# A two-layer RWKV/short-convolution and conformer backbone: where the context stages write their gate and receptance projections

## The chip, the cores and the metric

The kernel runs on one core of one Trainium2 chip. The metric is device time in microseconds (us) for one execution, taken as the median of several runs. A core has engines that each run their own queue in order: TensorE (PE in the profile, with its weight loads shown as PEld), VectorE (DVE), ScalarE (ACT), GpSimd (POOL) and SyncE (SP). In this kernel PE does the matrix products, DVE and ACT the elementwise work, and SP and POOL issue nearly all the transfers from memory.

## The reference, cut to what matters

There are 256 context tokens and 512 latent tokens of width 1024. Layer 0 normalises both, multiplies them with one wide matrix `ev_w_in` (eight blocks of 1024 columns: r, k, v, za, bg, cg, xb, zb), runs a bidirectional RWKV-7 recurrence over the context and then, from its final states, over the latent tokens, and joins that with a gated short convolution. Layer 1 is a conformer convolution module on the latent tokens alone.

```
rc, kc, vc, zac, bc, cc, xc, zbc = split(hc @ w_in)      # context
yac, S_f, S_b = rwkv_seq(prep(hc, rc, kc, vc), 0, 0)     # only the final states are used
r, k, v, za, bg, cg, xb, zb = split(h @ w_in)            # latent tokens
ya, _, _ = rwkv_seq(prep(h, r, k, v), S_f, S_b)
yb = bg * dwconv(cg * xb, sc_w)
y = concat(ya * silu(za), yb * silu(zb)) @ w_out
```

Of the context only k and v are needed (its outputs are thrown away). Of the latent tokens all eight blocks are needed; r and za are the two that the change moves.

## The kernel before

The recurrence is computed in chunks of 64 tokens. Inside a chunk a triangular system is inverted; between chunks a 64x64 state per head and direction is carried. Everything is float32, and a projection is made of three products of rounded halves (`mm3`), eight steps deep, so one latent projection of 128 columns by 512 tokens is 24 matmuls of 128x512, and one context projection is 24 of 128x256.

Layer 0 is a pipeline of twelve states. `sts[0]` to `sts[3]` are the context, two pairs of heads (a pair is 128 channels) in each; `sts[4]` to `sts[11]` are the latent tokens, one pair in each. For each `s` the kernel first writes the chain of `sts[s]` (`chain_ctx`, four steps, or `chain_lat`, eight steps: PE products `zo` and `uh`, ACT copies, a DVE update of the state H) and then the steps that prepare the next states, in the order of a string:

```
for x in STAGE[s >= 4]:
    if x == "S":
        solve(sts[s + 1])
    elif x == "M":
        merge(sts[s + 1])
    ...
    elif x == "P" and s < 10:
        sts.append(prep_ctx(s + 2) if s < 2 else prep_lat(s - 2))
    elif x == "L" and s < 10:
        light(sts[s + 2], st)
    elif x == "H" and s < 10:
        heavy(sts[s + 2], st)
    elif x == "F":
        fills(s + 1)
```

- **P** (`prep_ctx`, L391 and after): the keys and values of two pairs, for context (`pck`, `pcv`) and latent tokens (`plk`, `plv`) in one go, four context and four latent projections per stage. For a latent state (`prep_lat`) it is only loads of what was stored before.
- **L** (`light`): decay, in-context rate and normalised keys: short products (`ss`, `lw`, `la`), some eighteen DVE operations on 128x512 and as many on ACT, two passes, one for each direction z.
- **S** (`solve`): the inverse of the 32x32 diagonal blocks, 62 small DVE operations (L667, L669).
- **M** (`merge`): joins the 32x32 blocks to 64x64 with 64 small products (`uh`), two DVE transposes and copies. Its scratch tiles are the buffers `kd`, `a`, `P` of `light`, each with one copy, so a merge stands behind the `light` written before it.
- **H** (`heavy`): the products of a chunk with itself (`pac`, `pal`), masked by DVE (L610) into the tile E; transposed keys (`pbc`, `pbl`) and values (`pvc`, `pvl`) copied out by ACT.
- **F** (`fills`): the projections that nothing nearby needs: r (`plr`, which also has two DVE shifts) and za (`pza`, an ACT tanh at L802 and a DVE product at L803). `FILL_R` and `FILL_Z` fix which pair goes to which stage: `fills(1)` is za of pairs 1 to 3, `fills(2)` r of pair 2, `fills(3)` r of pair 3 and za of pairs 4 to 7, `fills(4)` r of pairs 4 to 7. Results are stored to memory and read back much later.
- **O**: `po`, for a latent state only.

Each half of a projection's weights is loaded by SP (256 KB), rounded by ACT (L128) and subtracted by DVE (L129) before PE can use it.

A scheduler in the framework lays the instructions of all engines out from the written order: what is written earlier has precedence, and later work is put into gaps where it expects the earlier to wait. So the written order is a ranking; the queues that come out of it are fixed when the program is built. The state `s` whose chain follows is written after all of this stage's steps.

Of the kernel before, what the change touches and what calls it, by code (L numbers as in the profile page):

```python
# [31 lines left out]
CONV_AFTER = (0, 2, 7, 6)  # L32
PA_ORDER = ((0, 1), (1, 0), (1, 1), (0, 0))
HEAVY = ("VBOAN", "ANBV")
STAGE = ("OFPLSMH", "OSPLMHFC")
FILL_R = (0, 0, 2, 3, 4, 4, 4, 4)
FILL_Z = (0, 1, 1, 1, 3, 3, 3, 3)
ZR = (slice(0, 64), slice(64, 128))
# [13 lines left out]
def kernel(ctx: ExitStack, tc: tile.TileContext, I: dict, out: bass.AP):  # L52
# [876 lines left out]
    for s in range(12):  # L929
# [7 lines left out]
        if s == 11:  # L937
            finish(st)
            break
        for x in STAGE[s >= 4]:  # L940
            if x == "S":
# [397 lines left out]
```

## Time and profile before

| | |
|---|---|
| median of 3 runs | 1439.53 us (1431.3 to 1440.98) |
| the profiled execution | 1434.6 us, span of its core 1432.5 us |
| PE busy | 1376.7 us, 96% |
| DVE busy | 983.0 us, 69% |
| ACT busy | 749.5 us, 52% |
| mean granted clock of PE | 0.982 |

The context stages lie between about 217 us and 525 us of the span, the latent stages of layer 0 from there to about 950 us, and then the output projection and layer 1, which keep PE full. A busy PE is no sign of PE at full speed: where the granted clock (row PEclk) is 0.50, the same matmul takes twice as long and counts as busy throughout.

### The profile page before, as it was taken

How to read it: one execution, taken by the hardware profiler on the slowest of the kernel's cores; microseconds unless marked ns; L12 is line 12 of the kernel's file. 1: busy time of each engine (PE TensorE's matmuls, PEld its weight loads, DVE VectorE, ACT ScalarE, POOL GpSimd, SP SyncE). 2: the span in 40 equal slices, each digit the busy share in tenths (PEclk: the TensorE clock that was granted, in tenths of full speed). 3: DMA queues.
4: the chain of work that ended last, by engine and by line, in shares of the span. 5: the costliest groups of instructions: out<-in, count | busy, mean ns of one | idle time of the engine just before them, and what ended most of it. 6: DMA issues, size and time to landing. Idle time of an engine off the chain costs nothing.

```text
span 1432.5 us, 29756 instructions
## 1 busy us (share of the span) xinstructions
PE 1376.7 (96%) x11921; PEld 1008.3 (70%) x11921; DVE 983.0 (69%) x2294; ACT 749.5 (52%) x1516; POOL 117.9 (8%) x246
## 2 busy tenths in 40 slices
PE   6899999999998998999999999999999999999998
PEld 1464677878776766666666666778777777788886
DVE  2675597568678989999999999656745545544333
ACT  4636355254555666756667565456753423464322
POOL 2023210000101101011010100010000000000000
PEclk9999999979898999999999999999999999999999
DMA  9754433222322221222222312358813303133322
GB/s 322 226 177 161 156 111 97 92 60 61 93 87 75 82 81 60 77 75 71 83 77 68 98 43 92 110 174 321 265 45 118 119 9 109 59 100 92 103 89 88
DMA packets 137626, 158.54 MB, mean 111 GB/s; under 512 B 15375, under 2 KB 104143, under 8 KB 137369
## 3 DMA queue, kind: packets, MB, share of 16 engines
q1 hardware_dynamic: 121104, 106.47, 23.7%
q0 software_dynamic: 15312, 48.99, 10.5%
q8 instruction: 94, 1.54, 0.4%
q10 hardware_dynamic: 1072, 1.19, 0.2%
q14 instruction: 44, 0.36, 0.1%
HBM read 138.33 MB, written 18.28 MB: 109 GB/s over the span
## 4 chain that ended last, share of the span: by engine, by line
PE 63%; DVE 14%; ACT 5%; issue 2%; DMA 0%; DVEq 0%; ACTq 0%
PE pu L57 12%; PE pz L57 6%; PE f L57 6%; PE o L57 5%; PE uh L57 4%; PE zol L57 4%; PE pcg L57 3%; PE pxb L57 3%; PE pza L57 3%; DVE E L610 2%; PE plk L57 2%; PE zoc L57 2%; PE pzb L57 2%; PE plv L57 1%; PE pac L57 1%
## 5 line engine op out<-in xcount | busy, mean ns | idle before, releaser
L57 PE MATMUL o<-wh,y 128*128 128x512 f32 x248 | 79.6, 397 | 0.0
L667 DVE TENSOR_TENSOR xtmpl<-Xl,Yl 128x126 f32<-128x126 f32 (+22 forms) x248 | 62.3, 251 | 2.8
L669 DVE TENSOR_TENSOR Yl<-Yl,xtmpl 128x126 f32<-128x126 f32 (+22 forms) x248 | 62.3, 251 | 2.7
L1152 ACT CAST ah<-a 64x512 fp32r<-64x512 f32 x32 | 19.8, 619 | 72.2 <-DVE a L1147 71.8
L57 PE MATMUL pal<-ARl,BKl 64*128 64x128 f32 x512 | 46.3, 300 | 10.7 <-DVE E L610 4.9
L57 PE MATMUL zol<-UV,E 64*64 64x64 f32 (+1 forms) x1024 | 54.2, 221 | 0.0
L57 PEld LDWEIGHTS o<-wh,y 128*128 128x128 f32 x248 | 45.9, 188 | 9.5
L57 PEld LDWEIGHTS pal<-ARl,BKl 64*128 64x128 f32 x512 | 36.4, 194 | 22.2 <-issue 7.2
L57 PE MATMUL zol<-Hl,ARl 64*64 64x64 f32 x896 | 50.2, 230 | 1.2 <-DVE Hl L782 1.0
L775 ACT COPY UV<-uh 64x128 f32<-64x128 f32 x128 | 33.2, 260 | 33.1 <-PE uh L57 25.6
L57 PE MATMUL o<-wl,y 128*128 128x512 f32 x124 | 49.4, 398 | 1.2 <-DVE wl L129 1.2
L57 PEld LDWEIGHTS zol<-Hl,ARl 64*64 64x64 f32 x896 | 35.0, 133 | 21.2 <-issue 17.0
L129 DVE TENSOR_TENSOR wl<-wr,wh 128x1024 fp32r<-128x1024 f32 x28 | 34.2, 1222 | 19.7 <-ACT wh L128 17.0
L57 PEld LDWEIGHTS uh<-UV,BKt 128*64 128x64 f32 x704 | 26.3, 137 | 28.7 <-ACT UV L775 23.0
L1147 DVE TENSOR_TENSOR a<-pu,a 128x512 f32<-128x512 f32 x16 | 11.0, 690 | 50.5 <-PE pu L57 48.2
L57 PEld LDWEIGHTS zol<-UV,E 64*64 64x64 f32 (+1 forms) x1024 | 42.4, 136 | 2.8 <-ACT UV L775 2.1
L610 DVE TENSOR_TENSOR E<-pal,maskE 128x512 f32<-128x512 f32 x64 | 42.9, 685 | 2.0 <-PE pal L57 1.2
L1107 DVE SCALAR_TENSOR_TENSOR pr<-px,dbe,What 119x512 f32<-119x512 f32 x32 | 22.6, 746 | 26.8 <-PE px L57 26.8
L782 DVE SCALAR_TENSOR_TENSOR Hl<-uh,PCl,HPl 128x64 f32<-128x64 f32 x112 | 26.5, 277 | 19.5 <-PE uh L57 8.6
L128 ACT CAST wh<-wr 128x1024 fp32r<-128x1024 f32 x28 | 29.6, 1056 | 19.7 <-DMA wr<-in_ev_w_out_dram 10.3
L886 POOL DMA_DIRECT2D mwr<-in_mod_w_dram x56 | 29.8, 537 | 112.8 <-PE uh L57 67.7
L57 PE MATMUL uh<-UV,BKt 128*64 128x64 f32 x704 | 36.3, 232 | 2.5 <-ACT UV L775 2.5
(947 smaller groups left out, 4230.9 us busy)
## 6 DMA issues: line engine op xcount, KB each, us to landing
mwr<-in_mod_w_dram POOLq DMA_DIRECT2D x56, 256.0 KB, 3.5
wr<-in_ev_w_out_dram SPq DMA_DIRECT2D x28, 512.0 KB, 5.1
ectx<-in_mod_w_dram SPq DMA_DIRECT2D x12, 512.0 KB, 5.2
wrk<-in_ev_w_in_dram SPq DMA_DIRECT2D x16, 256.0 KB, 3.1
wrv<-in_ev_w_in_dram SPq DMA_DIRECT2D x16, 256.0 KB, 4.1
wrr<-in_ev_w_in_dram SPq DMA_DIRECT2D x16, 256.0 KB, 2.7
wrza<-in_ev_w_in_dram SPq DMA_DIRECT2D x16, 256.0 KB, 2.8
wrcg<-in_ev_w_in_dram SPq DMA_DIRECT2D x16, 256.0 KB, 2.8
```

Of the source, the lines that this page charges most:

```text
L57: return T.matmul(o, lhsT, rhs, start=start, stop=stop)
L128: S.copy(hi, raw)
L129: env["lo"].tensor_tensor(out=lo, in0=raw, in1=hi, op=ALU.subtract)
L610: st["ev"].append(V.tensor_tensor(out=E[:, h, z * NLAT + c0 : z * NLAT + c0 + m, :], in0=pas[h], in1=maskE[:, z * (1 + h) : z * (1 + h) + ...
L667: V.tensor_tensor(out=tv, in0=X[:, :i, i : i + 1].to_broadcast([P, i, m]), in1=Y[:, i : i + 1, c0:].to_broadcast([P, i, m]), op=ALU.mult)
L669: V.tensor_tensor(out=Y[:, :i, c0:], in0=Y[:, :i, c0:], in1=tv, op=ALU.add)
L775: u_ = S.copy(UV[ZR[1 - h], i : 2 * nch - i : 2 * nch - 1 - 2 * i, ZR[h]], uh[ZR[1 - h], 0:2, :])
L782: h_ = V.scalar_tensor_tensor(out=Hn[:, z, :], in0=uh[:, 2 + z, :], scalar=PC[z][:, i : i + 1], in1=HP[:, z, :], op0=ALU.mult, op1=ALU.add)
L886: nc.gpsimd.dma_start(mws[q], I["mod_w"][layer, kt * P : (kt + 1) * P, c0 : c0 + 512])
L1107: V.scalar_tensor_tensor(out=pr[s][:NPROD], in0=px[s][:NPROD], scalar=dbe[:, 0:1], in1=What[:, n * 512 : n * 512 + 512], op0=ALU.add, op1= ...
L1147: V.tensor_tensor(out=a, in0=pp[1], in1=a, op=ALU.mult)
L1152: S.copy(ahl[s][hr], a[hr])
```

## The change

The order string of the context stages is changed; that of the latent stages and all else stays.

```
-STAGE = ("OFPLSMH", "OSPLMHFC")
+STAGE = ("OPLSMHF", "OSPLMHFC")
```

In each of the four context stages the r and za projections that were written ahead of the stage's keys and values are now written behind keys and values, preparation, inverse, merge and chunk products. No instruction is added or dropped but for how rows are grouped; the queues of PE, DVE, ACT, SP and POOL change their order from the first context stage on.

**PE, the first context stage, just ahead of the merge** (`uh`) of `sts[1]`, while `light` of `sts[2]` runs. `pbc` are the transposes of keys, `pck` a context key projection of the next stage, `pza` a za projection. Before:

```order
L57 MATMUL pck_3119<-hctx,whk_3108 128x256 x2
L57 MATMUL pck_3119<-hctx,wlk_3109 128x256
L57 MATMUL pck_3119<-hctx,whk_3114 128x256 x2
L584 MATMUL pbc_2828<-ident,BKc_2637 128x64
L584 MATMUL pbc_2827<-ident,BKc_2637 128x64
```

After:

```order
L57 MATMUL pza_2821<-hlh,wlza_2817 128x512
L57 MATMUL pza_2821<-hlh,whza_2816 128x512
L57 MATMUL pza_2821<-hll,whza_2816 128x512
L57 MATMUL pza_2821<-hlh,wlza_2817 128x512
L57 MATMUL uh_124<-amc_2587,ectx 32x32 x32
L584 MATMUL pbc_2705<-ident,BKc_2514 128x64
```

Between the first `lw` product of this `light` and the merge stood 24 `plr` matmuls and 14 narrow `pck`; now 42 `pza` stand there, and 30 more between the merge's first products and the next chain. The chain of `sts[0]` in turn has keys between its steps where it had `pza`.

**ACT, the same place**: casts (L128), tanh and exponentials of `light` (L513 to L533), and the four copies of transposed values (L640). Before:

```order
L527 ACTIVATE Pc_2594<-Pc_2594 128x528
L560 COPY BKc_2607<-BKc_2607 64x8x64
L529 COPY PCc_2599<-Pc_2594 128x8
L640 COPY UV_1044<-pvc_2786 64x8x64 x4
L520 ACTIVATE ac_2621<-lac_2618,hcol 128x256 x2
L526 ACTIVATE iPc_2626<-Pc_2624 128x512
```

After:

```order
L128 CAST whza_2816<-wrza_2815 128x512
L520 ACTIVATE ac_2498<-lac_2495,hcol 128x256 x2
L560 COPY BKc_2484<-BKc_2484 64x8x64
L526 ACTIVATE iPc_2503<-Pc_2501 128x512
L533 ACTIVATE kdc_2508<-ac_2498,oka,hka 128x256
L527 ACTIVATE Pc_2501<-Pc_2501 128x528
L533 ACTIVATE kdc_2508<-ac_2498,oka,hka 128x256
L529 COPY PCc_2506<-Pc_2501 128x8
L640 COPY UV_1044<-pvc_2663 64x8x64 x4
```

The value copies moved from ahead of the second direction's rate (`ac`) to behind the whole of it, and one cast of a za weight stands in their place.

**PE, the third context stage**, the first `light` of a latent state (products `ssl`, `lwl`, `lal`). Before, behind the last `pza` and at the head of the next chain (`zoc_0`):

```order
L57 MATMUL pza_4081<-hlh,wlza_4077 128x512
L57 MATMUL ssl_4129<-sql_4127,blk 128x512
L57 MATMUL lwl_4150<-tanhl_113,lwhl_4123 128x512
L57 MATMUL lwl_4150<-tanhl_113,lwll_4124 128x512
L57 MATMUL zoc_0_4471<-UV_1737,ectx 64x64 x8
L57 MATMUL plr_4658<-hlh,whr_4647 128x512
```

After, between the chain's own steps (`zoc_1`):

```order
L57 MATMUL zoc_1_3770<-UV_1044,ectx 64x64 x8
L57 MATMUL lwl_3944<-tanhl_113,lwhl_3917 128x512
L57 MATMUL lwl_3944<-tanhl_113,lwll_3918 128x512
L57 MATMUL lal_3949<-xal_115,lwhl_3917 128x512
L57 MATMUL zoc_1_3770<-cx,ectx 64x64 x8
L57 MATMUL lal_3949<-xal_115,lwll_3918 128x512
```

This `light` moved ahead by some four projections and lies inside the chain of `sts[2]`; the four `pza` that stood in front of it are now beside and behind it.

## The prediction

> **What bounds the kernel now.** I began with the page's engine totals and its slices.
>
> ```profile
> PE 1376.7 (96%) x11921; PEld 1008.3 (70%) x11921; DVE 983.0 (69%) x2294; ACT 749.5 (52%) x1516; POOL 117.9 (8%) x246
> PE   6899999999998998999999999999999999999998
> DVE  2675597568678989999999999656745545544333
> PEclk9999999979898999999999999999999999999999
> PE 63%; DVE 14%; ACT 5%; issue 2%; DMA 0%; DVEq 0%; ACTq 0%
> ```
>
> PE is busy nearly everywhere and holds most of the chain that ended last; transfers hold none of it. But the granted clock has three dents, all in the context stages, the only part that the change reorders. The next view is the busy time of each engine by stretches, cut at events: the chains' starts, and the first products of each `light`. Columns: stretch, its length, PE, PEld, DVE, ACT, POOL busy, granted clock, DMA share, GB/s.
>
> ```profile
> 253.00:288.00 35.00, 35.00 (x197) 30.16 (x195) 18.16 (x43) 11.12 (x20) 2.16 (x4) 1.00 0.32 98
> 288.00:320.00 32.00, 28.62 (x334) 23.26 (x335) 22.27 (x43) 18.93 (x39) 1.62 (x3) 0.79 0.20 59
> 364.00:395.00 31.00, 29.09 (x330) 22.10 (x329) 23.04 (x44) 19.83 (x40) 5.66 (x10) 0.84 0.31 90
> 395.00:427.00 32.00, 32.00 (x324) 23.87 (x323) 25.57 (x77) 17.34 (x41) 1.62 (x3) 0.95 0.27 79
> 427.00:457.00 30.00, 25.21 (x246) 19.43 (x244) 28.27 (x66) 15.18 (x27) 5.66 (x10) 0.82 0.31 97
> 457.00:525.00 68.00, 63.97 (x737) 48.16 (x734) 60.57 (x152) 44.95 (x90) 6.33 (x12) 0.98 0.26 77
> ```
>
> Keys and values (253 to 288) run PE without a hole and leave DVE half idle. Each `light` with the merge behind it (288 to 320, **gap A**; 364 to 395, **gap B**; 427 to 457, **gap C**) leaves PE holes, 3.38, 1.91 and 4.79 us, and a low clock. Cut finer, in 2 us:
>
> ```profile
> 302.00:304.00 2.00, 0.60 (x6) 0.40 (x4) 2.00 (x4) 1.98 (x5) 0.00 (x0) 1.00 0.00 0
> 304.00:306.00 2.00, 1.17 (x18) 0.82 (x18) 2.00 (x4) 1.70 (x3) 0.29 (x1) 1.00 0.00 0
> 306.00:308.00 2.00, 1.33 (x50) 1.33 (x52) 1.92 (x4) 1.76 (x4) 0.25 (x1) 0.58 0.49 123
> 308.00:310.00 2.00, 2.00 (x36) 1.94 (x34) 1.57 (x3) 0.58 (x1) 0.54 (x1) 0.50 0.06 18
> ...
> 322.00:324.00 2.00, 2.00 (x8) 1.61 (x8) 0.08 (x1) 1.94 (x5) 0.00 (x0) 0.65 0.00 0
> 382.00:384.00 2.00, 1.04 (x64) 1.04 (x64) 1.92 (x5) 1.97 (x4) 0.55 (x1) 1.00 0.32 61
> 384.00:386.00 2.00, 2.00 (x35) 1.96 (x29) 1.94 (x4) 0.66 (x2) 0.55 (x1) 0.71 0.20 78
> 398.00:400.00 2.00, 2.00 (x9) 1.65 (x8) 0.85 (x1) 1.96 (x4) 0.00 (x0) 0.88 0.00 0
> 442.00:444.00 2.00, 0.00 (x0) 0.00 (x0) 2.00 (x4) 1.21 (x2) 0.56 (x1) 1.00 0.33 121
> 446.00:448.00 2.00, 2.00 (x18) 1.53 (x15) 2.00 (x4) 0.64 (x2) 0.94 (x2) 0.57 0.05 18
> 458.00:460.00 2.00, 2.00 (x11) 1.25 (x12) 0.69 (x1) 1.96 (x5) 0.00 (x0) 0.52 0.00 0
> ```
>
> All three have one shape: DVE and ACT full, PE short of work for 4 us (1.77 of 4 us at A), then half clock for 12 to 16 us, with PE busy throughout. Lost by the clock, as (1 - clock) x 2 us summed over the windows: A 0.84 + 7 x 1.00 (308 to 322) + 0.70 = **8.5 us**; B 0.58 + 6 x 1.00 + 0.24 = **6.8**; C 0.86 + 5 x 1.00 + 0.96 = **6.8**. Why PE starved at A:
>
> ```profile
> 296.49 2.35 ACT L640 COPY UV<-pvc 64x512 f32<-64x512 f32 x4
> 298.87 0.84 ACT L520 ACTIVATE ac<-lac,hcol 128x256 f32<-128x256 f32 x2
> 303.95 0.50 PE L57 MATMUL pck<-hctx,whk 128*128 128x256 f32 x2 [1.40 <-ACT whk L128]
> 306.67 1.92 PE L57 MATMUL uh<-amc,ectx 32*32 32x32 f32 x64 [1.36 <-DVE amc L676]
> 319.85 0.37 PE L57 MATMUL zoc<-cx,ectx 64*64 64x64 f32 x2
> ```
>
> The fill ran out at a weight whose cast stands behind `light` in ACT's queue; then the merge waited for DVE. Nothing here waits for memory.
>
> [...]
>
> **The change part by part.** Unit prices, from the chain that ended last:
>
> ```profile
> 253.52 2.88 PE pck L57 x24
> 256.39 5.48 PE plk L57 x24
> L610 DVE TENSOR_TENSOR E<-pal,maskE 128x512 f32<-128x512 f32 x64 | 42.9, 685 | 2.0 <-PE pal L57 1.2
> ```
>
> So a latent projection costs PE 5.48/24 = 0.228 us a matmul, a context one 0.120; a 128x512 operation costs DVE 0.69.
>
> *Gap A.* The 72 `pza` leave the chain of `sts[0]` and fill gap A; keys take their place, so `light` starts 72 x 0.228 = 16.4 us earlier, about 272. Per chain step the fill stays 2 to 3 us; DVE has shifts instead of gate products ahead of its H update, which I price at 0.5 us in all (one 128x255 shift, bounds 0 and 2). In the gap, 288 to 319.85 took 31.85 us; less 3.38 idle and the 6.8 us of clock loss up to 319.85 leaves 21.7 us at full clock. After: plus 48 matmuls (72 `pza` for 24 `plr`), 10.9, less 19 `pck`, 2.3, is 30.3. PE then owes 24 `plr` and 19 `pck`, 7.7 us, to later. Net: A keeps its work and loses its holes and its dip, at most 8.5 + 3.4 = 11.9 us. Whether it does depends on the supply up to the merge.
>
> ```profile
> 288.02 0.70 PE L57 MATMUL lwc<-lorc,lwc2lwl 64*128 64x256 f32 x2
> 294.35 1.15 PE L57 MATMUL pvc<-ctr,vc 64*64 64x64 f32 x32
> 299.99 0.71 PE L584 MATMUL pbc<-ident,BKc 64*128 64x64 f32 x15
> ```
>
> Before, the merge came 18.65 us after the first `lw` (306.67 - 288.02). ACT's new order brings the second `ac` (298.87) forward by the value copies, 2.35 us, so it should come after about 16.5. PE's work up to there: 42 `pza`, 9.6 us, of which all but the last 6 have their weights cast before `light` or early in it; `lw` and `la`, which with six `plr` and eight chain products took 6.3 us (288.02 to 294.35), without those about 4.2; value and key products 1.15 + 0.71. Together 15.6, so about 1 us is left idle. **A: 11.9 - 1.0 - 0.5 = 10** (bounds 3, if it dips once more, and 11.9).
>
> *Gap B.* It gets the fill that A had, r of pair 2, then 18 of r of pair 3: 42 matmuls where 41 stood (24 `plr`, 17 `pza`), in the same places. **B: 0** (bounds -2 and +8.7, its whole loss).
>
> *Gap C and what follows.* Keys and values of a latent state are only loads, so with F behind, its `light` falls into the chain of `sts[2]`, and four `pza` cover the chunk products. The events between which I count are the second `zoc_0` of `sts[2]` and the product `pgv`:
>
> ```profile
> 395.07 1.12 PE L57 MATMUL zoc<-cx,ectx 64*64 64x64 f32 x16
> L973 PE MATMUL pgv<-ident,ss x1: 277/277/277, 525.4 to 525.4; 128*16 128x128 f32 x1
> ```
>
> 130.3 us, in which PE was busy 32.0 + 25.2 + 64.0 = 121.2, of that 8.5 clock loss (B's tail 1.7, C 6.8), so 112.7 of work; DVE 25.6 + 28.3 + 60.6 = 114.4. In both orders the same count of DVE instructions stands ahead of the H update that follows `pgv`. PE has 23 more matmuls to do in it (the debt of A), 5.2 us: 118; DVE about 116 (bounds 114 and 118). Two engines loaded alike, each waiting for the other in order: as in 457 to 525, where 64.0 of 68.0 were reached, 118 x 68/64 = 125.4, plus B's tail 1.7, is 127.1. Against 130.3 + 5.2 that gains **8.4** (bounds 0, no gain, and 14, no holes at all).
>
> *Latent stages, output, layer 1.* Their rows differ only in which chain step a conv projection falls on; DVE and PE are as full as before. 0, bounds -3 and +3.
>
> *Transfers.* SP's weight loads change order only, and two small state stores move ahead of one load each; the loads behind have over 10 us until needed. On POOL the store of the second `gza` of pairs 4 to 7 now stands behind loads for the next `light`, which wait for buffers; ACT's third gate needs that store. By my count it lands some 2 us ahead: cost 0, bound 3, inside C's.
>
> Sum: 10 + 0 + 8.4 = 18.4 from the profiled 1434.6 (span 1432.5 and 2.1 around it): **1416**. The three runs were 1431.3 to 1440.98, median 1439.53, 4.9 above the profiled one; the mean of all four is 1436.6, so I give 2 more, **1418**. About 1% is what a measurement here can tell from no change.
>
> **Rivals.**
> - *A dips again.* The merge's products are 32 wide, between key transposes, and at B 1.04 of 2 us busy ahead of the fall was enough. If PE's fill ends 2 us early, A pays as B does, 6.8 + 1.9 of 11.9: gain 2.7 instead of 10, 1424 by the profiled time. Against it: six `pza` directly ahead of the merge.
> - *C only moves.* `light` and `solve` both stand ahead of the merge of `sts[3]` in DVE's queue. If PE waits there as it did at 442 (0.00 of 2.00), dip and holes stay: gain 10, 1425. With A's dip too: 1432.
> - *Slower: DVE paces the chain.* In the chain of `sts[2]` the H updates now queue behind `light`. Two operations of 0.69 us ahead of an update that has no PE fill left beside it cost a step 1.4 us; if that holds for the 8 updates of the chains of `sts[2]` and `sts[3]` and for six of the eight mask groups (L610) beside them (14 x 1.4 = 19.6), PE is empty often enough for another dip like C's, 6.8 less the 1 that falls on holes. It decides from the point where a step has under 1.4 us of fill. 1434.6 - 10 + 25.4 = 1450. Against it: DVE has room, 25.6 of 32 us in 395 to 427.
> - *B also heals*, if it starts with its weights further ahead: 8.7 more, 1407.
> - *The fills don't move far enough*, the scheduler having put them where it likes: excluded for A and C by the rows, and just what holds for B.
>
> **How the numbers follow.** Forecast 0.45, A dips 0.22, C only moves 0.13, both 0.06, slower 0.09, B heals 0.05. The forecast's own range is 1410 to 1423. The range 1404 to 1440 takes in all but the slower case and half of the last; its upper end is "both", 1432, with a spread of runs. A full 1% faster is below 1420: three quarters of the forecast, a quarter of the next two, and B's: 0.47. Slower by 1%, above 1449: the slower case: 0.09, generously. The rest 0.44.
>
> **What would show it.** Clock 1.00 through the first `light` and merge, PE within 1 us of full there, and the chain of `sts[1]` starting near 303; the dip at B as before, near 367; no slice at half clock between there and `pgv`, which comes near 507. I am wrong if a dip stays in A, if the H updates of `sts[2]` are over 7 us apart, or if the time from `pgv` to the end (907 us) changes by over 3.

## The result, and the profile after

| | before | after |
|---|---|---|
| median (17 runs each) | 1437.58 us | 1427.01 us |
| lowest to highest | 1431.3 to 1440.98 | 1424.49 to 1432.3 |
| ratio, 95% interval | | 0.9932 [0.9921, 0.9944] |
| the profiled execution | 1434.6 us, clock 0.982 | 1429.56 us, clock 0.986 |

The change gains 0.7%, 10.6 us by the medians, where 18 were forecast. The two profiled executions differ by less, 5 us: that of before was 3.0 us below its median, that of after 2.6 above its own. From the page of the kernel after, the clock by slices:

```profile
PEclk9999999999799999999999999999999999999999
```

Of the three dents in the clock one is left in this coarse row. The same kernel by stretches (length, PE, PEld, DVE, ACT, POOL busy, granted clock, DMA share, GB/s), cut at its own events: gap A; gap B; the chain of `sts[2]` and the old place of gap C; the rest up to `pgv`.

```profile
272.50:304.50 32.00, 32.00 (x345) 24.19 (x344) 22.75 (x32) 24.67 (x47) 2.16 (x4) 1.00 0.31 91
350.00:382.00 32.00, 30.09 (x331) 23.30 (x330) 23.20 (x44) 20.08 (x40) 5.67 (x10) 0.81 0.29 88
382.00:448.00 66.00, 62.71 (x661) 47.44 (x661) 59.10 (x156) 40.17 (x81) 7.83 (x14) 0.96 0.32 92
448.00:514.00 66.00, 60.03 (x650) 45.90 (x649) 55.56 (x139) 38.60 (x80) 5.86 (x11) 0.95 0.27 78
```

Gap A has no hole and no dip: PE 32.00 of 32.00, clock 1.00. Gap B dips again, for 17.1 us where it was 13.7. The old dip at 442 to 460 is gone, but idle time and a lower clock stand in the last stretch. The same view, finer, shows B's dip, then two new ones behind it:

```profile
372.00:384.00 12.00, 12.00 (x138) 10.53 (x137) 4.83 (x8) 1.96 (x4) 0.00 (x0) 0.50 0.29 89
442.00:460.00 18.00, 17.66 (x283) 13.06 (x285) 17.09 (x58) 12.02 (x26) 1.09 (x2) 1.00 0.29 89
474.00:480.00 6.00, 1.87 (x33) 1.60 (x28) 6.00 (x15) 1.65 (x4) 0.77 (x2) 0.94 0.21 74
480.00:486.00 6.00, 6.00 (x33) 4.64 (x33) 4.62 (x12) 0.62 (x1) 0.00 (x0) 0.50 0.35 106
550.00:556.00 6.00, 2.45 (x28) 2.26 (x30) 6.00 (x19) 0.99 (x2) 0.00 (x0) 0.87 0.01 3
556.00:562.00 6.00, 6.00 (x35) 4.38 (x34) 5.15 (x23) 3.30 (x6) 0.00 (x0) 0.57 0.31 87
```

At 474 to 480 DVE is full (6.00 of 6) and PE has work for 1.87 us of 6; then the clock is at half up to 486.12. What happens there, in order of time, from PE's queue and from DVE's (start, length, operation, in brackets the wait before it and for whom):

```profile
452.13 0.80 PE L57 MATMUL lwl<-tanhl,lwhl 128*128 128x512 f32 x1
476.32 1.16 PE L57 MATMUL pal<-ARl,BKl 64*128 64x128 f32 x16 [1.95 <-DVE E L610]
479.65 2.08 PE L57 MATMUL pal<-ARl,BKl 64*128 64x128 f32 x16 [2.17 <-DVE E L610]
481.66 0.79 PE L57 MATMUL pcg<-hlh,wlcg 128*128 128x512 f32 x1
478.02 0.69 DVE L610 TENSOR_TENSOR E<-pal,maskE 128x512 f32<-128x512 f32 x1
478.62 0.29 DVE L669 TENSOR_TENSOR Yl<-Yl,xtmpl 128x128 f32<-128x128 f32 x1
479.62 0.69 DVE L129 TENSOR_TENSOR wlcg<-wrcg,whcg 128x512 fp32r<-128x512 f32 x1
```

The chunk products `pal` wait for DVE's masks (L610), which stand between the steps of `solve` (L667, L669). The fill, `pcg`, stands behind them in PE's queue, and it could not have run much earlier: the second half of its weight (`wlcg`) is made at 479.62, in the same DVE queue. So PE's work and its fill hang on one full engine. That `pal` belongs to a `light` whose first `lw` product ran at 452.13; before, that product ran at 484.59:

```profile
484.59 0.79 PE L57 MATMUL lwl<-tanhl,lwhl 128*128 128x512 f32 x1
```

Behind `pgv`, whose time is followed by the first product of layer 1 (`pu`):

```profile
L57 PE MATMUL pu<-wc010h,h1h x8: 389/397/504, 1031.5 to 1071.4; 128*128 128x512 f32 x8
```

```profile
L973 PE MATMUL pgv<-ident,ss x1: 271/271/271, 514.2 to 514.2; 128*16 128x128 f32 x1
L57 PE MATMUL pu<-wc010h,h1h x8: 389/398/504, 1026.6 to 1066.5; 128*128 128x512 f32 x8
```

The first row is before, the other two after: `pgv` to `pu` took 506.1 us (1031.5 - 525.4) and now takes 512.4. A second profile of the changed kernel has 512.0 and 1023.4, which is 511.4. From `pu` to the end it is 401.0 us in these three.

### The profile page after: what moved, and what is told of

Read it like the earlier page. It is cut to its first block, busy times and chain, and to the rows that moved or that the text cites. A ratio compares the mean times of both kernels' runs of the same rounds, so it can differ in the third digit from the quotient of the medians.

```text
span 1427.6 us, 29734 instructions
## 1 busy us (share of the span) xinstructions
PE 1372.9 (96%) x11921; PEld 1005.0 (70%) x11921; DVE 981.3 (69%) x2294; ACT 747.4 (52%) x1516; POOL 118.0 (8%) x246
## 4 chain that ended last, share of the span: by engine, by line
PE 70%; DVE 14%; ACT 7%; DMA 5%; issue 4%; POOL 0%; DVEq 0%; ACTq 0%; SPq 0%; POOLq 0%
PE pu L57 12%; PE pz L57 6%; PE f L57 6%; PE uh L57 4%; PE zol L57 4%; PE pcg L57 4%; PE plk L57 3%; PE plv L57 3%; PE pxb L57 3%; PE o L57 2%; PE pza L57 2%; PE pcv L57 2%; DVE E L610 2%; PE plr L57 2%; DMA wr<-in_ev_w_out_dram 2%
## 5 line engine op out<-in xcount | busy, mean ns | idle before, releaser
L667 DVE TENSOR_TENSOR xtmpl<-Xl,Yl 128x126 f32<-128x126 f32 (+22 forms) x248 | 62.6, 252 | 2.9
L669 DVE TENSOR_TENSOR Yl<-Yl,xtmpl 128x126 f32<-128x126 f32 (+22 forms) x248 | 62.3, 251 | 2.9
L610 DVE TENSOR_TENSOR E<-pal,maskE 128x512 f32<-128x512 f32 x64 | 43.2, 686 | 2.6 <-PE pal L57 2.4
L128 ACT CAST wh<-wr 128x1024 fp32r<-128x1024 f32 x28 | 29.6, 1057 | 20.8 <-DMA wr<-in_ev_w_out_dram 10.6
L57 PEld LDWEIGHTS uh<-Ol,E 64*64 64x64 f32 x512 | 19.9, 133 | 26.9 <-ACT Ol L769 20.4
## 6 DMA issues: line engine op xcount, KB each, us to landing
wr<-in_ev_w_out_dram SPq DMA_DIRECT2D x28, 512.0 KB, 5.0
ectx<-in_mod_w_dram SPq DMA_DIRECT2D x12, 512.0 KB, 4.7
```

The lines of the kernel that those rows point to most:

```text
L57: return T.matmul(o, lhsT, rhs, start=start, stop=stop)
L128: S.copy(hi, raw)
L610: st["ev"].append(V.tensor_tensor(out=E[:, h, z * NLAT + c0 : z * NLAT + c0 + m, :], in0=pas[h], in1=maskE[:, z * (1 + h) : z * (1 + h) + ...
L667: V.tensor_tensor(out=tv, in0=X[:, :i, i : i + 1].to_broadcast([P, i, m]), in1=Y[:, i : i + 1, c0:].to_broadcast([P, i, m]), op=ALU.mult)
L669: V.tensor_tensor(out=Y[:, :i, c0:], in0=Y[:, :i, c0:], in1=tv, op=ALU.add)
```

## The experiments

Unless said otherwise, an edit writes one string per context stage, with `N = "OPLSMHF"` for the new order and `O = "OFPLSMH"` for the old:

```
-STAGE = ("OFPLSMH", "OSPLMHFC")
+STAGE = (N, O, O, O, "OSPLMHFC")      # here: first stage new
-        for x in STAGE[s >= 4]:
+        for x in STAGE[min(s, 4)]:
```

| stages 1 to 4 | median us | ratio to before, 95% interval | median clock of its runs |
|---|---|---|---|
| before, O O O O | 1436.0 to 1437.4 | | 0.982 |
| N O O O | 1428.3 | 0.9944 [0.9924, 0.9964] | 0.9855 |
| O O N O | 1433.1 | 0.9974 [0.9959, 0.9988] | 0.9845 |
| O O O N | 1445.7 | 1.0059 [1.0038, 1.0080] | 0.977 |
| O O N N | 1440.4 | 1.0032 [1.0018, 1.0046] | 0.9805 |
| N O N O | 1423.7 | 0.9914 [0.9889, 0.9939] | 0.991 |
| N N N O | 1420.7 | 0.9884 [0.9856, 0.9912] | 0.992 |
| N N N N (the change) | 1427.7 | 0.9932 [0.9913, 0.9951] | 0.9875 |

**First stage alone** (N O O O).

> Only the first context stage is written in the new order; the other three are as before. Theory (the whole gain is gap A): the hole and the clock dip of 302 to 322 go, worth the 8.5 us of clock and 3.4 us of idle time less what stays, and the 24 receptance matmuls taken from gap A (5.5 us) are paid back before gap C; so the time falls by about 10 us, ratio 0.992 to 0.995, the same as the whole change, and the dips at B and C stay where they were, each some 13 us earlier. Rival (the later stages carry a part of their own): this kernel gains clearly less than the whole change, 3 to 7 us, ratio 0.995 to 0.998, because the latent-state light of the third stage was to give 3 to 8 us.

It gains 8.1 us and its profile shows why (gap A, gap B, gap C):

```profile
272.00:304.00 32.00, 32.00 (x358) 23.99 (x356) 23.25 (x37) 24.44 (x48) 2.15 (x4) 1.00 0.28 84
368.00:392.00 24.00, 22.58 (x266) 18.58 (x265) 13.98 (x21) 11.69 (x21) 1.66 (x3) 0.64 0.23 67
432.00:452.00 20.00, 15.41 (x217) 11.78 (x217) 15.11 (x28) 6.69 (x12) 2.19 (x4) 0.66 0.32 100
```

A is healed; B and C dip earlier and are otherwise of the same kind. Term A holds. That the gain is about that of the whole change doesn't show that the later stages do nothing: below, the third gains and the fourth loses.

**Third and fourth stage** (O O N N).

> The first two context stages are as before, the third and fourth are in the new order: term C of the prediction alone. Theory (C only moves): dip C at 442 to 460 goes and another of about the same size comes some 30 to 40 us later, where the masks of the chunk products stand in DVE's queue with the inverse; the time from the second chain product of the third state (395 us) to the first chain product of the latent part (525 us) stays 130 within 3 us, ratio 0.998 to 1.002. Rival (the forecast's size was right, and only the 5.2 us debt of gap A ate it): that stretch shortens by 6 to 8 us, ratio 0.994 to 0.996.

Neither: slower, by 4.0 us in the medians and 4.6 by the ratio. The old dip is gone (442 to 460 at 1.00), another, half as large, stands at 486 to 500:

```profile
442.00:460.00 18.00, 16.05 (x224) 12.39 (x224) 16.77 (x45) 9.78 (x17) 2.17 (x4) 1.00 0.36 101
486.00:500.00 14.00, 10.10 (x78) 7.83 (x77) 12.23 (x30) 3.19 (x7) 1.10 (x2) 0.76 0.29 86
```

From `zoc<-cx` of `sts[2]` (397.57) to `pgv` (526.9) it took 129.3 us against 130.3, so "the dip only moves" describes this stretch; most of the slower time comes behind `pgv`, where `pu` follows 513.3 us later instead of 506.1.

**Fourth stage left old** (N N N O).

> The new order in the first three context stages, the old one in the fourth. Theory 1 (the new hole at 472 to 488 comes from the fourth stage, where fills stand behind the masks): the hole goes, its 5 us of idle time and 5 us of clock come on top, 8 to 10 us faster than the whole change, ratio 0.986 to 0.989. Theory 2 (the hole is a matter of DVE having masks, inverse and light in one stretch, whatever the order of the fourth stage): it only moves, ratio 0.992 to 0.994 as the whole change.

```profile
424.00:460.00 36.00, 32.69 (x407) 24.53 (x407) 32.97 (x94) 19.73 (x39) 2.71 (x5) 1.00 0.32 97
472.00:488.00 16.00, 15.85 (x80) 12.46 (x79) 16.00 (x42) 11.77 (x21) 3.49 (x6) 1.00 0.34 99
550.00:562.00 12.00, 9.69 (x79) 7.48 (x81) 11.02 (x40) 4.64 (x8) 0.00 (x0) 0.72 0.15 44
```

Theory 1 holds: from 424 to 488 the clock is 1.00 and the hole at 472 is gone, with DVE just as full (16.00 of 16). The time is 7 us below the whole change, a little less than the 8 to 10 expected. That `light` runs at 471 instead of 452, with `pcg` and `pxb` as fill beside it. `pgv` to `pu` is 508.8 us.

**The change once more.**

> The whole change once more, for a second profile. If the 6.3 us that the stretch from the first latent chain (pgv) to the end was longer in the first profile belong to the change, they are there again within 2 us (913 us against 907); if they are chance of one execution, the stretch is nearer to 907. The dip at B and the hole at 472 to 488 are there again in both cases, ratio 0.992 to 0.994.

From `pgv` to `pu` it is 511.4 us: the loss is the change's own. The hole at 472 to 480 is there again, with the same two waits of 1.95 and 2.17 us, and so is B's dip, though each of the two dips is 1.7 us of lost clock smaller than in the first profile.

**First and third stage** (N O N O).

> The new order in the first and the third context stage, the old one in the second and the fourth. Theory (term C was sized right, and the fourth stage took it back): about as fast as the kernel with three new stages, 1.0 to 1.3% below before (ratio 0.987 to 0.990), no slice at half clock between 400 and 512 us, the dip at B as before. Rival (the second stage brought what the three-stage kernel gained over the first stage alone): only the first stage's gain is left, ratio 0.993 to 0.996, and a dip stays near 435 to 450 us.

1423.7 us, between the two by its time. Its profile speaks for the theory: the clock is 1.00 from 440 to 460 and from 472 to 488, where the dips of before and of the change stood, and `pu` follows `pgv` after 507 us. The difference from N N N O, 3 us, is inside the intervals, so what the second stage is worth stays open.

**Fourth stage alone** (O O O N) and **third stage alone** (O O N O).

> Only the fourth context stage is written in the new order. Theory (this stage alone costs: its light and chunk products come forward into the last context chain, PE stands behind masks with its fill in the queue behind them, a new dip follows, and the latent stages lose 4 to 6 us): 5 to 9 us slower than before, ratio 1.0035 to 1.006. Rival (the loss needs the debt of the earlier stages): within 2 us of before, ratio 0.9985 to 1.0015.

> Only the third context stage is written in the new order: term C of the prediction without the fourth stage and without the debt of gap A. Theory (the term was sized right for this stage): the dip at 442 to 460 goes with its holes, 4 to 8 us faster than before, ratio 0.9945 to 0.997. Rival (the dip only moves, as in the kernel with the third and fourth stage new): within 2 us of before, 0.9985 to 1.0015.

The fourth stage costs 8.3 us by itself, so it needs no debt of the others. The part of the theory on the latent stages does not hold: `pgv` to `pu` takes 508.2 us, 2 more than before and not 4 to 6. A stretch of its profile and the longest wait in it:

```profile
488.00:502.00 14.00, 8.50 (x67) 6.27 (x67) 14.00 (x30) 5.59 (x11) 3.41 (x6) 0.76 0.29 89
496.67 2.08 PE L57 MATMUL pal<-ARl,BKl 64*128 64x128 f32 x16 [5.43 <-DVE E L610]
```

The third stage gains 4.3 us by the medians, 3.7 by the ratio: the dip goes, and a smaller one appears in the first latent stage:

```profile
426.00:464.00 38.00, 32.96 (x364) 25.07 (x365) 35.28 (x94) 18.85 (x34) 3.27 (x6) 1.00 0.39 116
560.00:570.00 10.00, 7.19 (x59) 5.24 (x59) 10.00 (x36) 3.65 (x6) 0.00 (x0) 0.83 0.19 54
```

By the ratio it lies just short of the range given to the theory. The interval, 1.7 to 5.9 us of gain, excludes the rival but for its edge, and excludes the 8.4 us of term C clearly.

**What in the fourth stage costs**: N N N and `"OPLSMFH"`. This puts the fills ahead of the chunk products (H) alone; they stay behind `light`, inverse and merge. The expectation below has them ahead of the merge too, which the string does not do.

> The new order in the first three stages; the fourth has its fills ahead of merge and chunk products but behind light and inverse. Theory 1 (what costs in the fourth stage is that its light runs ahead of the fills, into the last context chain, which makes masks and inverse fall together on DVE): as slow as the whole change, ratio 0.992 to 0.995, with a dip between 460 and 500. Theory 2 (what costs is that the chunk products stand ahead of the fills in PE's queue): as fast as the three-stage kernel, ratio 0.987 to 0.990.

```profile
478.99 2.08 PE L57 MATMUL pal<-ARl,BKl 64*128 64x128 f32 x16 [3.71 <-DVE E L610]
472.00:484.00 12.00, 8.29 (x55) 6.09 (x54) 11.90 (x31) 4.31 (x9) 1.10 (x2) 0.72 0.42 124
```

1428.6 us, ratio 0.9947 [0.9928, 0.9966]: as the whole change, with the first `lw` product of that `light` still at 452.63 and the hole still there. So theory 2 falls: it is not the fill's place behind the chunk products that costs. What is left is its place behind `light`, inverse and merge, which lets that `light` run early; which of the three counts was not tried.

**Dense and narrow matmuls at gap A**, in the kernel before, in its old order. Products that nobody reads are added ahead of the merge and between its two groups (shortened, `...` stands for what is left out; the counts are in the expectations below):

```
+        r2 = V.transpose(R2, R1)
+        dummy(..., r2, sts[-1]["BK"][1][:, :, ZR[1]])   # ahead of the merge's first group
...
             last = mm(pg[low[z], ...], ...)
+        dummy(..., last)                                # between its two groups
# dense:  mm(du, hlat[0][:, j, 0:P], hlat[0][:, j, :], True, True)            128x512
# narrow: 4 x mm(du[0:64, ...], ident[0:64, 0:64], ident[0:64, 0:64], ...)    64x64
```

> The kernel before in its old order, with eight extra 128x512 matmuls that nobody reads at gap A: two in 32-bit form (about 0.6 us each) ahead of the merge, six in the rounded form (0.23 us each) between the merge's two groups of products; some 2.6 us of added work, of which the 1.4 us of PE's wait ahead of the merge can hide a part. Theory (dip A is a matter of how long PE gets no full-width matmuls, and the dip, not the hole, holds most of term A): the clock stays at or near 1.00 from 304 to 322, the 8.5 us of lost clock go, and the time falls by 4 to 8 us, ratio 0.9945 to 0.997. Rival (the clock follows the longest hole or the load over tens of us): the dip stays and the time rises by 1 to 3 us, ratio 1.000 to 1.002.

> The same places filled with narrow matmuls that nobody reads: 24 of 64x64 in each, about 1.5 us a place at full clock, so PE is as busy as in the kernel with dense ones. Theory (only full-width matmuls keep the clock): the dip stays, the added matmuls run at half clock, the time rises by 1 to 5 us, ratio 1.001 to 1.0035. Rival (any busy PE keeps the clock, the holes alone drop it): the dip goes as with dense ones, the time falls by 4 to 8 us.

Dense, then narrow; in each two windows and the two groups of added products (the profile has two rows for each 32-bit one: x4 for two, x48 for 24):

```profile
306.00:312.00 6.00, 3.96 (x9) 1.79 (x9) 5.92 (x11) 4.46 (x8) 0.54 (x1) 0.72 0.12 33
312.00:326.00 14.00, 14.00 (x276) 11.90 (x277) 6.47 (x11) 4.54 (x10) 0.54 (x1) 1.00 0.21 63
308.64 3.30 PE L58 MATMUL dumc<-BKc,ident 128*128 128x512 f32 x4
313.27 1.65 PE L58 MATMUL dumc<-hlh 128*128 128x512 f32 x6
```

```profile
306.00:312.00 6.00, 4.59 (x42) 4.41 (x42) 5.92 (x11) 3.82 (x7) 0.54 (x1) 0.67 0.17 46
312.00:342.00 30.00, 30.00 (x333) 26.94 (x333) 8.36 (x15) 7.83 (x17) 0.54 (x1) 0.50 0.09 27
307.89 5.27 PE L58 MATMUL dumc<-BKc,ident 64*64 64x64 f32 x48
314.93 5.38 PE L58 MATMUL dumc<-ident 64*64 64x64 f32 x48
```

Both lose the clock near 308, behind the same 2.10 us wait for a key weight. With dense products it is back after 3.4 us ((1 - 0.72) x 6 / 0.5), 1.7 us lost instead of 8.5, and stays at 1.00 through the merge. With narrow ones PE is busy for 30.00 of 30.00 us and the clock stays at 0.50 all that time, through a few 128x256 products too. It came back at 342.2, behind 3.8 us of nothing but 128x512 key projections, of which this is the first:

```profile
338.44 0.80 PE L58 MATMUL plk<-hlh,whk 128*128 128x512 f32 x1
```

The times are 1434.0 us (0.9986 [0.9971, 1.0000], clock 0.988) and 1442.9 (1.0056 [1.0037, 1.0076], clock 0.978). So at gap A the kind of matmul decided when the clock came back (after 3.4 us with dense ones, after 34.1 with narrow ones, from 308.08 to 342.2), as the theory had it, but the sizes were missed on both sides. The dense kernel gains 2 us, with an interval that reaches no change, and not 4 to 8: its added products took 3.30 + 1.65 us where 2.6 had been estimated, and the wait ahead of them grew from 1.40 to 2.10. The narrow one loses 7 and not 1 to 5: its products took 5.27 + 5.38 us where the estimate of 1.5 us a place comes to 6 at half clock, and the full-width key projections behind which the clock came back stood later (338.44 instead of 322.12). Neither account was carried to the end.

**Dense matmuls at gap B**, six between the merge's groups, on N N N O.

> The new order in the first three context stages, and six extra rounded 128x512 matmuls that nobody reads (1.4 us) between the two groups of merge products at gap B. Theory: the dip at B (8.5 us of lost clock in the three-stage kernel's profile, 368 to 392) goes or is cut to under 3 us, and the time falls another 4 to 7 us below the three-stage kernel, to a ratio of 0.983 to 0.986. Rival (B's dip comes from the wait ahead of the merge, 1.1 us, which stays): no change but the added 1.4 us, ratio 0.988 to 0.990.

```profile
366.00:372.00 6.00, 3.90 (x89) 2.79 (x87) 5.92 (x11) 5.63 (x11) 1.12 (x2) 1.00 0.24 68
372.00:392.00 20.00, 20.00 (x313) 15.69 (x306) 16.16 (x46) 13.89 (x32) 0.54 (x1) 1.00 0.20 61
```

In the profiled execution the dip at B is gone, though the wait ahead of the merge stays (3.90 of 6). The time says nothing of it: 1424.3 us, 0.9931 [0.9904, 0.9958], no faster than without. Its eight executions had clocks from 0.986 to 0.995, so the dip probably came back in some, which no trace shows. Inconclusive on the time.

**Needed work in the same place**: first and third stage new, fourth old, and the second `"OPLFSMH"`, its fills behind `light` but ahead of inverse and merge.

> The first and third stage in the new order, the fourth in the old one, and the second with its fills behind light but ahead of inverse, merge and chunk products. In the queue of PE this puts 26 instead of 14 full-width matmuls directly ahead of the merge at gap B and five between its two groups, all of them needed work. Theory (B dips for want of full-width matmuls around the merge): dip B is cut to under 3 us and the time is 3 to 8 us below the three-stage kernel's, ratio 0.983 to 0.987. Rival (the weights of these fills come no earlier, so PE waits for their casts instead): the dip stays, ratio 0.988 to 0.992.

```profile
366.00:384.00 18.00, 17.56 (x286) 13.73 (x285) 13.49 (x25) 13.03 (x24) 2.30 (x4) 1.00 0.41 117
434.00:442.00 8.00, 6.80 (x140) 5.43 (x141) 6.74 (x18) 2.78 (x5) 1.08 (x2) 0.79 0.44 133
```

B's dip is gone, a short one is left at 436. The wait of 1.1 us ahead of the merge is gone too, so this run doesn't tell apart what the filled wait and the full-width work within the merge did. The four executions took 1413.5 to 1416.4 us, median 1413.8, ratio 0.9849 [0.9826, 0.9873], at clocks of 0.995 to 0.997. This version beats both kernels. That it is below N N N O rests on intervals that overlap a little (0.9856 to 0.9912).

## Why the prediction was wrong, step by step

Forecast 1418, measured 1427: the direction held, and a little over half of the size came. The rival "C only moves", which had 0.13, gave nearly this number (1425), but not for what happened: it had PE wait ahead of the merge of `sts[3]`, and there the dip went. That its number fits is luck.

- **Term A, 10 us: right.** No hole, no dip, and the first stage alone gains 8.1 us. The product that stood at 319.85 (`zoc<-cx` of `sts[1]`) is at 306.10; the forecast was near 303. The marker ahead of the chain of `sts[2]` stands 13.0 us earlier than at 395.07, of 15.5 that A should give while its 5.5 us of fill are owed; the traces differ by 1.3 us at their first chain already, and B, from its first `lw`, took 1.0 longer:

```profile
382.06 1.12 PE L57 MATMUL zoc<-cx,ectx 64*64 64x64 f32 x16
```

- **Term B, 0: right.** The dip stayed, at 370 instead of 367.
- **Term C, 8.4 us: wrong.** The stretch to `pgv` was to shrink from 130.3 to 127.1 us; it took 132.1 (514.2 - 382.06) and 130.7 in the second profile. By the forecast's own sum, with the 5.2 us of A's debt, the term came to 3.4 and 4.8 us. The step that failed is the one that scaled the whole stretch by 64.0 of 68.0, as if the holes were spread thin and no dip could follow. In the first profile the clock took 5.9 us of the stretch where 1.7 were allowed (3.4 in a new dip at 479, 2.5 in B's tail), and holes took 9.3 where the scaling gives 7.4. One part did come: the third stage takes the old dip away and gains 3.7 us alone. The other part, what the fourth stage does, was not priced apart. Its fill written behind `light`, inverse and merge lets that `light` run at 452 instead of 484, though all else came only 11 to 13 us earlier; its masks then fall on the steps of `solve`, and PE stands behind `pal`. The slower rival had named the masks (L610), but as steps of 1.4 us over six groups; here waits of 1.95 and 2.17 us, or one of 5.43 with the fourth stage alone, came ahead of a dip. The chain itself was not paced by DVE, as that rival had it: the H updates of `sts[2]` stood 6.6, 6.6 and 6.1 us apart, under the 7 named as a sign.
- **Latent stages, 0 with bounds of 3: wrong.** They lost 6.3 and 5.3 us in the two profiles. Clock lost at 550 to 562 is 3.4 of it ((1 - 0.87) x 6 + (1 - 0.57) x 6), again behind two waits of `pal` for masks; N N N O has that dip too, with 508.8 us in all. Four `pcg` matmuls not yet done at `pgv` are 0.9 us. The cause of the other 1 to 2 us is open. All four profiles with the third and fourth stage new have 511 to 513 us, but N N N O with dense matmuls at B, its fourth stage old, has 510.7 as well. The rows of the latent stages were compared and found alike, but not at what moment they would meet a full DVE.
- **The sum of what came**: -13.0 to 382, +1.8 to `pgv`, +6.3 to `pu`, together -4.9, which is the difference of the two spans (1432.5 and 1427.6).
- **The reading of the clock** was right in kind and too weak in use. Over the 129 executions that the experiments brought of the ten orders without added products, time follows the granted clock: 1410.7 us + 1427 us x (1 - clock) fits them with a spread of 2.3 us and a correlation of 0.95. Each order's median less that second part lies between 1407 and 1413 us. The orders do the same work; most of their difference is how much of it runs at half clock. A sum kept in dips lost and dips made, stage by stage, would have asked what the fourth stage makes.

The clock also keeps to a grid, which the prediction's reading missed. In the trace of the kernel before and in the first of the changed one, every fall and every return of the clock stands a whole number of steps of 3.413 us from the others of its trace (191.15 us are 56 of them, by the edges below). In six of the experiments' traces the edges that windows of 2 us place agree with it to 0.05 us: with the fourth stage alone the clock falls at 309.28, 387.76, 449.20 and 493.60, which is 23, 41 and 54 steps behind the first. In every window that holds whole dips the loss is 1.7 us for each dip or a multiple of it (8.5, 6.8 and 6.8 in the kernel before are 5, 4 and 4 steps, 17.1, 13.7 and 13.7 us at half clock). The first profile of the changed kernel, at four of its edges:

```profile
370.00:370.20 0.20, 0.20 (x20) 0.20 (x16) 0.19 (x1) 0.20 (x1) 0.00 (x0) 0.66 0.87 307
387.00:387.20 0.20, 0.20 (x2) 0.10 (x2) 0.20 (x1) 0.20 (x2) 0.00 (x0) 0.68 0.00 0
479.20:479.40 0.20, 0.00 (x0) 0.00 (x0) 0.20 (x1) 0.00 (x0) 0.00 (x0) 0.72 0.00 0
561.20:561.40 0.20, 0.20 (x1) 0.20 (x2) 0.17 (x2) 0.20 (x1) 0.00 (x0) 0.98 0.00 0
```

By the shares of these windows the clock fell at 370.06, came back at 387.13, fell at 479.29 and came back at 561.21: 5, 32 and 56 steps behind the first. How many steps a given stretch costs differed from one execution to the next: B's dip took five steps in the first profile of the change and four in the second. Over 62 executions of the unchanged kernel the clock was 0.976 to 0.987.

## What to carry to other kernels

Read the granted clock beside PE's busy time, and look at a stretch of small matmuls as at a gap: with narrow products added at gap A, PE was busy for 30.00 of 30.00 us at a clock of 0.50. Try some needed full-width work in such places: the fastest version here, 1413.8 us at clocks of 0.995 to 0.997, had five such matmuls between the merge's two groups at gap B and 26 instead of 14 directly ahead of it. Reordering to fill one hole moves the next stage's work forward as well, so price each stage of a repeated order apart, and ask of each which engine its earlier work will meet. Test a change of order stage by stage; here the first and third gained and the fourth took part of it back. Compare medians for this: the two profiles of the change differ by a step of the clock's grid, 1.7 us, in each of the dips at 370 and 479.

## What the runs showed of the hardware

With narrow matmuls added (64x64, beside the merge's 32x32 and a few of 128x256) PE was busy for 30.00 of 30.00 us without the clock rising from 0.50. In three dips it came back behind 128x256 and 128x512 ones alone, after 2.5 us of them in the kernel before (128x256 from 320.89, 128x512 from 322.12, the clock at 323.4), 3.8 with narrow products added (338.44 to 342.2) and 4.0 in the first profile of the change (383.11 to 387.13), each time at a step of the grid. At half clock the 128x512 matmuls of a projection started 0.43 us apart, at full clock 0.23, so 1.9 times as far and not the full twice. At gap A of the kernel before the clock fell at 306.3, with whole holes of 1.40 and 1.36 us, and it was 0.50 from 308 to 322 with PE 2.00 of 2.00 busy. At gap B of the changed kernel it fell with a longest whole hole of 1.10 us. The last full-width matmul ahead of the fall and the first merge product, in the first profile of the changed kernel and in the second, there with the window in which the clock fell:

```profile
367.00 0.40 PE L57 MATMUL plr<-hll,whr 128*128 128x512 f32 x1
369.14 1.31 PE L57 MATMUL uh<-amc,ectx 32*32 32x32 f32 x64 [1.10 <-DVE amc L676]
```

```profile
367.90 0.40 PE L57 MATMUL plr<-hll,whr 128*128 128x512 f32 x1
370.03 1.20 PE L57 MATMUL uh<-amc,ectx 32*32 32x32 f32 x64 [1.09 <-DVE amc L676]
372.00:384.00 12.00, 12.00 (x142) 10.33 (x141) 5.68 (x9) 2.74 (x5) 0.54 (x1) 0.54 0.30 89
```

The clock fell at 370.06 in the first and near 373.0 in the second: 2.7 and 4.7 us behind the end of the last full-width matmul, with the same program. Whether the width in rows, in columns or in elements counts was not tried.
